# Gate and up stage of a gated feed-forward block: casts and first sums taken from GpSimd, one product copied by ScalarE, one weight load later

## The chip, the cores and the metric

The kernel runs on one core of a Trainium2 chip as one launch. The metric is the device time of one execution in microseconds (us). The times of the kernel before are the median of three runs. One further execution was taken by the hardware profiler, and all durations and start times below come from that one, counted from the start of its span.

TensorE does the matrix products and writes into PSUM banks. VectorE (DVE in the trace), ScalarE (ACT) and GpSimd (POOL) work on SBUF tiles, and DVE and ACT also read PSUM. SyncE (SP) issues the DMAs. Each engine takes its instructions in program order, and an instruction whose inputs aren't there holds up what stands behind it on that engine.

## The reference, cut to what matters

Two encoder layers over 1024 tokens of width 1024. Each has a mixer (attention), a layer norm, the feed-forward block below, a second layer norm and a gated embedding. The change lies in the first half of the feed-forward block, in both layers:

```python
def conv_ffn(x, w_gate, w_up, conv_w, conv_b, w_down):
    a = x @ w_gate                    # 1024 x 2816
    u = x @ w_up                      # 1024 x 2816
    c = conv_b                        # plus a convolution of width 3 over tokens
    for j in range(3):
        c = c + conv_w[j] * ap[:, j:j + S]    # ap: a, padded by one token
    return (gelu(c) * u) @ w_down
```

## The kernel before, in words

**Products.** Each matrix product is done in three matmuls (lines 159 to 161), since every operand is split into a rounded high part and the low rest: high by high, high by low, low by high. The high part is a cast (`CAST` on ACT, `TENSOR_SCALAR` on POOL), the low part is a subtraction on DVE (line 142).

**Seven products.** Gate and up are done as 2 x 2 blocks with seven block products in place of eight (the Strassen-Winograd scheme). A weight set, `Weights`, holds two 128-column strips of one matrix; the sets alternate, gate (even m) and up (odd m), and there are 22 in a layer (m = 0 to 21). From its quarters a00, a01, a10, a11 come four sums: the first sums s1 = a10 + a11 and s3 = a00 - a10, and, on DVE, s2 = s1 - a00 and s4 = a01 - s2. Each of a00, s2, s3, s1, a01, a11, s4 is split (14 instructions of 128x512 a set, seven casts and seven subtractions). Here `split` sends the casts of s3, a01 and a11 to POOL and the other four to ACT, and `steps` puts the two first sums on POOL for all sets from the third on (m >= 2).

**Products on TensorE.** `Products.product` issues 12 matmuls of 128x512 for one block. a00 and s2 go into the two halves of one PSUM tile `pa` (two banks, of which there are two such tiles), the others each into one of four banks `pb`. `read` sums finished blocks: m is a copy of a00's product (ACT, line 1342), u2 = m + s2's, u3 = u2 + s3's, then c11 and so on, on DVE (line 1332). A bank comes free for a later product when the last sum that reads it is done.

**The first pair.** Sets 0 and 1 are ready before the inputs are all there, and run `ahead`: their products come in the order a00, a01, then s1, s4, s2, s3, a11 for both sets by turns. So u2 of these two sets, which reads s2's half of `pa`, is due late, beside the last splits of the inputs (`xt.finish`, 128x1024 instructions on DVE and ACT). c11's second half of the work (line 1353) is one addition a set on POOL.

**Order.** `ffn` issues everything by a counter n of products; in the dictionary of line 1503 stand the steps at which a piece of `todo` (sums, then seven splits) is taken for set 2. A scheduler then fixes each engine's order from the program. Weights come by DMA on SP's queue (`load`, two of 512 KB), into a ring of 36 units that the sums and u tiles share.

Of the kernel before, what the change touches and what calls it, by code (L numbers as in the profile page):

```python
# [12 lines left out]
ALU = mybir.AluOpType  # L13
# [19 lines left out]
def tile_hybrid_encoder(  # L33
# [32 lines left out]
    nc = tc.nc  # L66
# [12 lines left out]
    def unit(s, shape, dt=F32):  # L79
        return up.tile(shape, dt, tag="u", name=nm(s))  # L80
# [26 lines left out]
    def rtile(s, shape, dt=F32R):  # L107
        return region[0].tile(s, shape, dt)
# [7 lines left out]
    def mid2(s, shape, dt=F32):  # L116
        return sm.tile(shape, dt, tag="mid2", name=nm(s), bufs=4)
# [10 lines left out]
    def f32(ap):  # L128
        return ap.bitcast(F32)
# [8 lines left out]
    def pool_copy(o, i):  # L138
        nc.gpsimd.tensor_scalar(o, i, 1.0, 1.0, op0=ALU.mult, op1=ALU.mult)  # L139

    def lo_part(lo, src, hi):
        nc.vector.tensor_tensor(lo, src, f32(hi), op=ALU.subtract)  # L142

    def split(raw, h, l, hi=None, lo=None):
        if hi is nc.scalar:
            nc.scalar.copy(h, raw)  # L146
        else:
            pool_copy(h, raw)
        (lo or nc.vector).tensor_tensor(l, raw, f32(h), op=ALU.subtract)  # L149

    def load_split(dram, shape, s, make=runit, hi=None, lo=None):
        r = region[0].raw(s + "r", shape)
        nc.sync.dma_start(out=r, in_=dram)
        h, l = make(s + "h", shape), make(s + "l", shape)
        split(r, h, l, hi, lo)
        return h, l
# [161 lines left out]
    def add(o, a, b, op=ALU.add, eng=None):  # L318
        return (eng or nc.vector).tensor_tensor(f32(o), f32(a), f32(b), op=op)

    def split_value(v, h, l, hi=None):
        if hi is nc.gpsimd:
            pool_copy(h, v)
        else:
            nc.scalar.copy(h, v)  # L325
        lo_part(l, v, h)
# [316 lines left out]
    class BlockB:  # L643
# [7 lines left out]
        def steps(self):  # L651
            out = []
            if self.pr % 2 == 0:
                out += [self.g.load] + [lambda t=t: self.g.project(t) for t in range(NT)]
            out.append(self.load)
            out += [lambda t=t: self.project(t) for t in range(NT)]
            return out
# [249 lines left out]
    class MixTiles:  # L907
# [4 lines left out]
        def seven(self, t):  # L912

            mr = region[0].raw("mr", [P, NK, P])
            nc.sync.dma_start(out=mr[:, 0:7, :], in_=mix[self.i].rearrange("k p q -> p k q")[:, 0:7, t * P:(t + 1) * P])
            two = [runit("mhl", [P, 2, 4, P]) for _ in range(2)]
            for j, m in enumerate(two):
                n = 4 - j
                split(mr[:, 4 * j:4 * j + n], m[:, 0, 0:n], m[:, 1, 0:n])
            self.m[t] = mr, two  # L920
# [342 lines left out]
    class Weights:  # L1263
# [22 lines left out]
            for step in steps:  # L1286
                step()

        HI = {"s3", "a01", "a11"}

        def split(self, name, raw=None):
            raw = name in ("a00", "a01") if raw is None else raw
            hl = region[0].raw("w", [P, 2, 4, P], F32R) if raw else rtile("w", [P, 2, 4, P])
            self.h[name], self.l[name] = hl[:, 0], hl[:, 1]
            split_value(self.v[name], hl[:, 0], hl[:, 1], nc.gpsimd if name in self.HI else None)

        def steps(self):

            return [lambda: self.sums(nc.gpsimd)] + [lambda n=n: self.split(n) for n in Products.ORDER]

    class Products:

# [26 lines left out]
        def read(self):  # L1329

            def plus(o, a, name):
                nc.vector.tensor_tensor(o, a, self.o[name], op=ALU.add)  # L1332
            out = []
            had = set(x for x, _ in self.sums)
            for name, need in list(self.sums):
                before = {"m": (), "u2": ("m",), "u3": ("u2",), "c11": ("u3",), "c00": ("m",) if self.ahead else ("u2",), "c10": ("u3", "c11"), "k5": (),
                          "c01": ("c11",)}[name]
                if any(x not in self.o for x in need) or any(x in had for x in before):
                    continue
                if name == "m":  # L1340
                    self.m = mid2("m", [P, 512])
                    nc.scalar.copy(self.m, self.o["a00"])
                elif name == "u2":
                    u = unit("u", [P, 2, 512])
                    self.u2, self.u3 = u[:, 0, :], u[:, 1, :]
                    plus(self.u2, self.m, "s2")
                elif name == "u3":
                    plus(self.u3, self.u2, "s3")
                elif name == "k5":
                    self.c11 = mid2("c11", [P, 512])  # L1350
                    nc.scalar.copy(self.c11, self.o["s1"])
                elif name == "c11" and self.ahead:
                    nc.gpsimd.tensor_tensor(self.u2, self.u2, self.c11, op=ALU.add)
                    nc.vector.tensor_tensor(self.c11, self.u3, self.c11, op=ALU.add)
                elif name == "c11":
                    self.c11 = mid2("c11", [P, 512])
                    plus(self.c11, self.u3, "s1")
                    plus(self.u2, self.u2, "s1")
                elif name == "c00":
                    if self.c00 is None:  # L1360
                        self.c00 = self.m
                    plus(self.c00, self.m, "a01")
                elif name == "c10":
                    plus(self.u3, self.u3, "a11")
                    self.c10 = self.u3
                elif name == "c01":
                    plus(self.u2, self.u2, "s4")
                    self.c01 = self.u2
                had.discard(name)
                out.append(name)  # L1370
            self.sums = [x for x in self.sums if x[0] in had]
            return out
# [14 lines left out]
    def ffn(i, w, xt, late, prefetch):  # L1387
# [3 lines left out]
        def new_c():  # L1391
            late_c.append(big("c", [P, 2, 1024]))
# [51 lines left out]
        def finished(n):  # L1444
            if n >= 0:
                m = order[n][0]
                for name in pr[m].read():
                    use(pr[m], m, name)
# [12 lines left out]
        todo = []  # L1461
        for n, (m, name) in enumerate(order):
            finished(n - 1)
            pr[m].product(name)
            if n == 0:
                c00 = unit("c00", [P, 2, 512])
                for a in range(2):
                    pr[a].go_ahead(c00[:, a])
                for a in range(2):
                    sums[a] = w[a].sums()  # L1470
                    sums[a][0]()
                    w[a].split("s1")
            if n == 1:
                late()
                new_c()
                temps = [late_c[0][:, a, :].rearrange("p (k q) -> p k q", k=2) for a in range(2)]
            if n == 2:
                for a in range(2):
                    sums[a][1]()
                    sums[a][2]()  # L1480
                    w[a].split("s4")
            if n == 3:
                for a in range(2):
                    xt.finish("t2", a)
                for a in range(2):
                    w[a].split("s2", True)
            if n == 4:
                for a in range(2):
                    xt.finish("t3", a)
                for a in range(2):  # L1490
                    sums[a][3]()
                    w[a].split("s3")
            if n == 5:
                for a in range(2):
                    xt.finish("t4", a, temps[a])
            if n == 6:
                w[0].split("a11")
                w[1].split("a11")
                w[2].load()
            if n == 7:  # L1500
                w[3].load()
                todo = w[2].steps()
            for _ in range({8: 1, 10: 2, 11: 1, 12: 1, 13: 3}.get(n, 0)):
                todo.pop(0)()
            if m >= 2 and m + 1 < NF:
                j = Products.ORDER.index(name)
                if j == 0:
                    todo = w[m + 1].steps()
                    todo[0]()
                    if m + 2 < NF:  # L1510
                        w[m + 2].load()
                todo[j + 1]()
            if m == NF - 1:
                down.ahead(Products.ORDER.index(name))
# [98 lines left out]
    for i in range(2):  # L1613
        if i == 0:
            w, mt, oT = mixer_ab(xt)
        else:
            tc.keep_in_program_order(nc.scalar.preload_act_table_set("natural_log_exp_and_others"))
            w, mt, oT = mixer_c(xt, late)
# [107 lines left out]
```

## Time and profile before

| | us |
|---|---|
| median of three runs (lowest, highest) | 3049.84 (3045.6, 3051.87) |
| the profiled execution, its own time | 3047.42 |
| its span, first to last instruction | 3045.1 |
| mean granted TensorE clock | 0.993 of full speed |
| gate and up stage, both layers together (815 to 1232 and 2300 to 2718) | 835.0, of it TensorE busy 808.9 |

The time of an execution is its span and some 2.3 us around it. In a row of a timeline the first number is the start, the second the duration; consecutive instructions of one engine overlap a little, so that the distance from start to start is shorter than the duration. "[9.24 <-DVE u L1332]" means that the engine sat idle for 9.24 us before, and that an instruction of DVE at line 1332, which writes a tile u, ended that. Tiles in the trace carry no numbers: `pa<-xb,w` is a matmul into a tile pa from an input tile and a weight tile.

### The profile page before, as it was taken

To read this page: it belongs to the slowest core of one execution; us is meant where nothing else is said; L and a number is where in the kernel's file an instruction comes from. 1 tells how busy PE (TensorE), PEld (TensorE's weight loads), DVE (VectorE), ACT (ScalarE), POOL (GpSimd) and SP (SyncE) were. 2 spreads that over 40 slices of the span, in tenths; PEclk is the share of its full clock that TensorE was granted. 3 is DMA by queue.
4 is the path that set the end of the run, shared out by engine and by line. 5 is a ranking of instruction groups with operands and counts; after the bars stand their busy time and mean duration, and the time that the engine had idled before them with its cause. 6 is when DMAs were issued, how large, how long until landed. Compare 5 with 4: busy or idle time off the path is not lost.

```text
span 3045.1 us, 42940 instructions
## 1 busy us (share of the span) xinstructions
PE 2949.2 (97%) x15456; PEld 2533.8 (83%) x15456; DVE 2308.2 (76%) x4022; ACT 1318.1 (43%) x2806; POOL 963.6 (32%) x1484
## 2 busy tenths in 40 slices
PE   8999999999989999999999999999998999999999
PEld 7888989887768888888888999998776788888887
DVE  6666477876898888688648777777769888877874
ACT  4555477761222222345225555555413222234431
POOL 4444544243232222000225555554332222210012
PEclk9999999999999999999999999999999999999999
DMA  3000100034223332734111100001431333346331
GB/s 123 29 28 19 38 29 8 8 130 134 90 98 104 104 104 100 276 133 169 63 59 34 34 32 29 28 18 56 155 129 69 115 104 104 104 163 244 115 127 66
DMA packets 119715, 272.10 MB, mean 89 GB/s; under 512 B 11344, under 2 KB 35024, under 8 KB 119504
## 3 DMA queue, kind: packets, MB, share of 16 engines
q1 hardware_dynamic: 119504, 269.37, 26.0%
q8 instruction: 122, 2.00, 0.3%
q14 instruction: 89, 0.73, 0.1%
HBM read 196.46 MB, written 72.88 MB: 88 GB/s over the span
## 4 chain that ended last, share of the span: by engine, by line
PE 74%; DVE 15%; ACT 3%; issue 3%; POOL 3%; DMA 2%; SPq 0%; DVEq 0%; ACTq 0%; POOLq 0%
PE pb L159 5%; PE pb L161 5%; PE pb L160 5%; PE xt L164 5%; PE pp L159 4%; PE s L588 4%; PE pp L161 4%; PE pp L160 4%; PE pd L159 4%; PE pd L161 4%; PE pd L160 4%; PE pa L159 2%; PE pg L159 2%; PE pg L161 2%; PE pg L160 2%
## 5 line engine op out<-in xcount | busy, mean ns | idle before, releaser
L142 DVE TENSOR_TENSOR ptl<-xt,pth 128x512 fp32r<-128x512 f32 (+2 forms) x384 | 239.7, 652 | 60.2 <-ACT pth L399 43.6
L159 PE MATMUL pp<-wh,xth 128*128 128x384 f32 x768 | 266.1, 347 | 8.0 <-ACT wh L146 7.6
L160 PE MATMUL pp<-wl,xth 128*128 128x384 f32 x768 | 258.8, 337 | 2.0 <-DVE wl L149 1.8
L161 PE MATMUL pp<-wh,xtl 128*128 128x384 f32 x768 | 257.9, 336 | 0.0
L440 ACT ACTIVATE e<-s,nmx 128x1024 f32<-128x1024 f32 x192 | 214.7, 1120 | 81.7 <-DVE nmx L838 59.0
L160 PE MATMUL pd<-wd,gd 128*128 128x512 f32 x616 | 239.9, 389 | 0.2 <-DVE wd L142 0.2
L159 PE MATMUL pd<-wd,gd 128*128 128x512 f32 x616 | 239.8, 389 | 0.0
L161 PE MATMUL pd<-wd,gd 128*128 128x512 f32 x616 | 239.7, 389 | 0.0
L325 ACT CAST w<-ws 128x512 fp32r<-128x512 f32 x132 | 81.1, 621 | 336.6 <-PE pb L161 281.0
L164 PE MATMUL xt<-ident,e 128*128 128x128 f32 x1440 | 198.1, 274 | 9.6 <-POOL e L740 3.0
L159 PE MATMUL pb<-xt,w 128*128 128x512 f32 x528 | 207.1, 392 | 0.0
L160 PE MATMUL pb<-xt,w 128*128 128x512 f32 x528 | 206.9, 392 | 0.0
L161 PE MATMUL pb<-xt,w 128*128 128x512 f32 x528 | 206.6, 391 | 0.0
L1149 ACT CAST gd<-gr 128x512 fp32r<-128x512 f32 x154 | 96.0, 623 | 214.9 <-PE pd L161 176.1
L164 PEld LDWEIGHTS xt<-ident,e 128*128 128x128 f32 x1440 | 163.5, 141 | 30.4 <-ACT sq L870 5.9
L896 POOL TENSOR_SCALAR rs<-mv 128x1 f32<-128x1 f32 x32 | 9.3, 291 | 547.7 <-DVE mv L895 547.1
L139 POOL TENSOR_SCALAR w<-ws 128x512 fp32r<-128x512 f32 x44 | 33.4, 760 | 467.0 <-PE pa L161 416.8
L142 DVE TENSOR_TENSOR gd<-gr,gd 128x512 fp32r<-128x512 f32 x154 | 106.1, 689 | 77.1 <-ACT gd L1149 77.1
L142 DVE TENSOR_TENSOR w<-ws,w 128x512 fp32r<-128x512 f32 x176 | 152.4, 870 | 5.2 <-ACT w L325 3.1
L159 PEld LDWEIGHTS pp<-wh,xth 128*128 128x128 f32 x768 | 144.6, 188 | 13.3 <-ACT wh L146 8.2
L838 DVE TENSOR_REDUCE nmx<-s 128x1 f32<-128x1024 f32 x128 | 150.4, 1214 | 2.6 <-PE s L588 2.6
L159 PE MATMUL pb<-xb,w 128*128 128x512 f32 x352 | 139.9, 397 | 9.8 <-DVE u L1332 5.7
(292 smaller groups left out, 8905.2 us busy)
## 6 DMA issues: line engine op xcount, KB each, us to landing
gr<-gated SPq DMA_DIRECT2D x76, 512.0 KB, 3.7
gated<-c SPq DMA_DIRECT2D x90, 256.0 KB, 3.5
wf<-in_w_gate_dram SPq DMA_DIRECT2D x44, 512.0 KB, 4.1
wf<-in_w_up_dram SPq DMA_DIRECT2D x44, 512.0 KB, 4.2
wd<-in_w_down_dram SPq DMA_DIRECT2D x44, 512.0 KB, 5.5
wr<-in_w_c_dram SPq DMA_DIRECT2D x32, 384.0 KB, 3.3
gated<-u SPq DMA_DIRECT2D x44, 256.0 KB, 2.2
pes<-peo SPq DMA_DIRECT2D x64, 128.0 KB, 1.9
```

The lines of the kernel that those rows point to most:

```text
L139: nc.gpsimd.tensor_scalar(o, i, 1.0, 1.0, op0=ALU.mult, op1=ALU.mult)
L142: nc.vector.tensor_tensor(lo, src, f32(hi), op=ALU.subtract)
L159: nc.tensor.matmul(o, lhsT=lh, rhs=rh, start=start, stop=False)
L160: nc.tensor.matmul(o, lhsT=lh, rhs=rl, start=False, stop=False)
L161: nc.tensor.matmul(o, lhsT=ll, rhs=rh, start=False, stop=stop)
L164: nc.tensor.transpose(o, in_=i, identity=ident)
L325: nc.scalar.copy(h, v)
L440: nc.scalar.activation(dst, s, AF.Exp, bias=negmax, scale=1.0, accum_out=l)
L588: nc.tensor.matmul(s[:, kh * 512:kh * 512 + 512], lhsT=qt[:, hl, i, :], rhs=self.ks[kh][:, j, :], start=hl == 0, stop=hl == 1)
L838: nc.vector.tensor_reduce(out=nmx, in_=s, axis=AX.X, op=ALU.max, negate=True)
L896: nc.gpsimd.tensor_scalar(rs, mv[:, 1:2], 1.0, LN_EPS, op0=ALU.mult, op1=ALU.add)
L1149: nc.scalar.copy(g[:, 0], rg)
```

## The change

Five edits, all in the gate and up stage. (1) `split` casts on ACT in all cases. (2) `steps` takes an engine: the first sums of sets 2 and 3 are done by DVE, those of later sets by POOL as before. (3) In the first pair, u2 is first a copy by ACT of s2's product, to which DVE adds m. (4) The addition of the first pair at line 1353 goes from POOL to DVE. (5) Set 3 is loaded at n = 10 in place of 7, behind the first steps of set 2.

```diff
--- before.py
+++ after.py
@@ -1286,17 +1286,15 @@
             for step in steps:
                 step()
 
-        HI = {"s3", "a01", "a11"}
-
         def split(self, name, raw=None):
             raw = name in ("a00", "a01") if raw is None else raw
             hl = region[0].raw("w", [P, 2, 4, P], F32R) if raw else rtile("w", [P, 2, 4, P])
             self.h[name], self.l[name] = hl[:, 0], hl[:, 1]
-            split_value(self.v[name], hl[:, 0], hl[:, 1], nc.gpsimd if name in self.HI else None)
-
-        def steps(self):
-
-            return [lambda: self.sums(nc.gpsimd)] + [lambda n=n: self.split(n) for n in Products.ORDER]
+            split_value(self.v[name], hl[:, 0], hl[:, 1])
+
+        def steps(self, eng):
+
+            return [lambda: self.sums(eng)] + [lambda n=n: self.split(n) for n in Products.ORDER]
 
     class Products:
 
@@ -1343,14 +1341,18 @@
                 elif name == "u2":
                     u = unit("u", [P, 2, 512])
                     self.u2, self.u3 = u[:, 0, :], u[:, 1, :]
-                    plus(self.u2, self.m, "s2")
+                    if self.ahead:
+                        nc.scalar.copy(self.u2, self.o["s2"])
+                        add(self.u2, self.u2, self.m)
+                    else:
+                        plus(self.u2, self.m, "s2")
                 elif name == "u3":
                     plus(self.u3, self.u2, "s3")
                 elif name == "k5":
                     self.c11 = mid2("c11", [P, 512])
                     nc.scalar.copy(self.c11, self.o["s1"])
                 elif name == "c11" and self.ahead:
-                    nc.gpsimd.tensor_tensor(self.u2, self.u2, self.c11, op=ALU.add)
+                    nc.vector.tensor_tensor(self.u2, self.u2, self.c11, op=ALU.add)
                     nc.vector.tensor_tensor(self.c11, self.u3, self.c11, op=ALU.add)
                 elif name == "c11":
                     self.c11 = mid2("c11", [P, 512])
@@ -1498,14 +1500,15 @@
                 w[1].split("a11")
                 w[2].load()
             if n == 7:
+                todo = w[2].steps(nc.vector)
+            if n == 10:
                 w[3].load()
-                todo = w[2].steps()
             for _ in range({8: 1, 10: 2, 11: 1, 12: 1, 13: 3}.get(n, 0)):
                 todo.pop(0)()
             if m >= 2 and m + 1 < NF:
                 j = Products.ORDER.index(name)
                 if j == 0:
-                    todo = w[m + 1].steps()
+                    todo = w[m + 1].steps(nc.vector if m == 2 else nc.gpsimd)
                     todo[0]()
                     if m + 2 < NF:
                         w[m + 2].load()
```

ScalarE in layer one, from the last casts of the inputs on. In the program order before (xt are inputs, w weights of set 2 and ws their sums, c_10441 a scratch tile that then holds gate values):

```order
L325 CAST xt_2492_10513<-t_2426_10113 128x1024
L325 CAST xt_2498_10540<-c_10441 128x1024
L1399 ACTIVATE c_10441<-c_2464_10384,convt 128x512
L325 CAST xt_2500_10546<-c_10441 128x1024
L325 CAST w_10641<-wf_10573 128x512
L325 CAST w_10644<-ws_10606 128x512
L325 CAST w_10694<-ws_10606 128x512
```

and after, where w_10518 to w_10570 belong to sets 0 and 1, and pa_10371 and pa_10443 hold s2's products of these:

```order
L325 CAST w_10518<-ws_10386 128x512
L325 CAST w_10522<-ws_10392 128x512
L325 CAST w_10567<-wf_10261 128x512
L325 CAST w_10570<-wf_10296 128x512
L325 CAST xt_2498_10540<-c_10441 128x1024
L1401 ACTIVATE c_10441<-c_2464_10384,convt 128x512
L325 CAST xt_2500_10546<-c_10441 128x1024
L325 CAST w_10643<-wf_10573 128x512
L325 CAST w_10720<-wf_10573 128x512
L325 CAST w_10646<-ws_10602 128x512
L1345 COPY u_10608<-pa_10371 128x512
L1345 COPY u_10623<-pa_10443 128x512
```

Five of these casts came from POOL (w_10518, w_10522, w_10567, w_10570 and w_10720). All stand ahead of the cast of set 2's s2 (w_10646), and behind that stand the two copies out of PSUM.

VectorE at the same place, from the low parts of set 2's first weights on. Before (u is u2 of sets 0 and 1, pb_10628 s3's product):

```order
L142 TENSOR_TENSOR w_10718<-wf_10573,w_10718 128x512
L142 TENSOR_TENSOR w_10641<-wf_10573,w_10641 128x512
L319 TENSOR_TENSOR ws_10606<-ws_10606,wf_10573 128x512
L319 TENSOR_TENSOR ws_10607<-wf_10573,ws_10606 128x512
L1332 TENSOR_TENSOR u_10612<-m_10397,pa_10371 128x512
L1332 TENSOR_TENSOR u_10626<-m_10466,pa_10443 128x512
L142 TENSOR_TENSOR w_10644<-ws_10606,w_10644 128x512
L1332 TENSOR_TENSOR u_10612<-u_10612,pb_10628 128x512
```

and after:

```order
L142 TENSOR_TENSOR w_10643<-wf_10573,w_10643 128x512
L142 TENSOR_TENSOR w_10720<-wf_10573,w_10720 128x512
L319 TENSOR_TENSOR ws_10602<-wf_10574 128x512
L319 TENSOR_TENSOR ws_10603<-wf_10573,wf_10574 128x512
L319 TENSOR_TENSOR ws_10602<-ws_10602,wf_10573 128x512
L319 TENSOR_TENSOR ws_10603<-wf_10573,ws_10602 128x512
L142 TENSOR_TENSOR w_10646<-ws_10602,w_10646 128x512
L319 TENSOR_TENSOR u_10608<-u_10608,m_10397 128x512
L319 TENSOR_TENSOR u_10623<-u_10623,m_10466 128x512
L1330 TENSOR_TENSOR u_10608<-u_10608,pb_10626 128x512
```

The two first sums are new here, and the additions into u read no PSUM.

VectorE some 30 instructions on, where set 3 is made. Before (pb_10785 is s3's product of set 2):

```order
L319 TENSOR_TENSOR ws_10753<-ws_10753,wf_10590 128x512
L319 TENSOR_TENSOR u_10626<-c_10441,u_10626 128x512
L319 TENSOR_TENSOR ws_10754<-wf_10590,ws_10753 128x512
L142 TENSOR_TENSOR w_10763<-wf_10590,w_10763 128x512
L142 TENSOR_TENSOR w_10780<-ws_10753,w_10780 128x512
L142 TENSOR_TENSOR w_10798<-ws_10754,w_10798 128x512
L142 TENSOR_TENSOR w_10815<-ws_10753,w_10815 128x512
L1332 TENSOR_TENSOR u_10783<-m_10766,pa_10740 128x512
L142 TENSOR_TENSOR w_10834<-wf_10590,w_10834 128x512
L1332 TENSOR_TENSOR u_10783<-u_10783,pb_10785 128x512
```

and after (pb_10787 is that product):

```order
L319 TENSOR_TENSOR ws_10755<-wf_10640 128x512
L319 TENSOR_TENSOR u_10623<-c_10441,u_10623 128x512
L319 TENSOR_TENSOR ws_10755<-ws_10755,wf_10639 128x512
L319 TENSOR_TENSOR ws_10756<-wf_10639,wf_10640 128x512
L319 TENSOR_TENSOR ws_10756<-wf_10639,ws_10755 128x512
L142 TENSOR_TENSOR w_10765<-wf_10639,w_10765 128x512
L142 TENSOR_TENSOR w_10782<-ws_10755,w_10782 128x512
L1330 TENSOR_TENSOR u_10785<-m_10768,pa_10742 128x512
L142 TENSOR_TENSOR w_10800<-ws_10756,w_10800 128x512
L1330 TENSOR_TENSOR u_10785<-u_10785,pb_10787 128x512
```

Two first sums came in, two low parts went behind, and the read of s3's product still ends the piece. On TensorE the product behind it, set 2's s4, is issued after ten matmuls of set 3's a00 in place of four.

## Rows read from the trace of the kernel before

**Rows 1.** The page: busy time by engine (1), the chain by engine (4).
```profile
PE 2949.2 (97%) x15456; PEld 2533.8 (83%) x15456; DVE 2308.2 (76%) x4022; ACT 1318.1 (43%) x2806; POOL 963.6 (32%) x1484
...
PE 74%; DVE 15%; ACT 3%; issue 3%; POOL 3%; DMA 2%; SPq 0%; DVEq 0%; ACTq 0%; POOLq 0%
```

**Rows 2.** TensorE's waits, whole program: line, releaser, us in total, times, longest.
```profile
PE pa L159 <- DVE u L1332: 18.5, 2, 9.2
...
PE pb L159 <- DVE u L1332: 5.7, 2, 2.9
...
PE pa L159 <- ACT m L1342: 1.7, 4, 0.5
```

**Rows 3.** Windows, layer one: engines' busy us (instructions), granted clock, DMA share, GB/s.
```profile
839.00:848.20 9.20, 0.05 (x1) 0.00 (x0) 9.07 (x10) 3.52 (x5) 4.85 (x4) 0.77 0.01 3
848.20:854.10 5.90, 5.81 (x14) 4.34 (x15) 5.33 (x8) 0.54 (x1) 2.90 (x2) 0.50 0.01 3
854.10:873.90 19.80, 19.80 (x88) 16.12 (x86) 19.80 (x28) 8.53 (x12) 5.86 (x5) 1.00 0.26 96
873.90:881.30 7.40, 4.54 (x14) 3.42 (x14) 7.40 (x12) 2.33 (x3) 3.09 (x2) 0.78 0.69 251
...
882.00:1218.00 336.00, 334.80 (x1462) 272.81 (x1462) 291.47 (x423) 95.97 (x140) 88.79 (x86) 1.00 0.30 102
```

**Rows 4.** Timeline of TensorE around both gaps: start us, duration us, line, form, [idle before].
```profile
838.66 0.39 PE L161 MATMUL pb<-xt,w 128*128 128x512 f32 x1
848.29 0.77 PE L159 MATMUL pa<-xb,w 128*128 128x512 f32 x1 [9.24 <-DVE u L1332]
...
873.67 0.39 PE L159 MATMUL pa<-xb,w 128*128 128x512 f32 x1
876.91 0.50 PE L159 MATMUL pb<-xb,w 128*128 128x512 f32 x1 [2.86 <-DVE u L1332]
```

**Rows 5.** Timeline of VectorE over the same stretch, layer one.
```profile
829.25 1.29 DVE L319 TENSOR_TENSOR ws<-wf,wf 128x512 f32<-128x512 f32 x2
830.45 1.22 DVE L319 TENSOR_TENSOR c<-xb,t 128x1024 f32<-128x1024 f32 x1
832.18 2.12 DVE L142 TENSOR_TENSOR w<-ws,w 128x512 fp32r<-128x512 f32 x2 [0.51 <-POOL w L139]
...
837.93 2.31 DVE L142 TENSOR_TENSOR xt<-c,xt 128x1024 fp32r<-128x1024 f32 x1
...
843.56 1.46 DVE L142 TENSOR_TENSOR xt<-c,xt 128x1024 fp32r<-128x1024 f32 x1
...
846.14 0.68 DVE L319 TENSOR_TENSOR ws<-ws,wf 128x512 f32<-128x512 f32 x1
...
847.46 1.28 DVE L1332 TENSOR_TENSOR u<-m,pa 128x512 f32<-128x512 f32 x2
...
851.71 1.75 DVE L1354 TENSOR_TENSOR c<-u,c 128x512 f32<-128x512 f32 x1 [0.57 <-POOL u L1353]
...
870.96 1.09 DVE L319 TENSOR_TENSOR u<-c,u 128x512 f32<-128x512 f32 x1
...
876.19 0.67 DVE L1332 TENSOR_TENSOR u<-u,pb 128x512 f32<-128x512 f32 x1
```

**Rows 6.** The tile ws, GpSimd's groups: duration ns min/median/max, first and last.
```profile
L139 POOL TENSOR_SCALAR w<-ws x22: 620/620/2030, 830.1 to 1216.1; 128x512 fp32r<-128x512 f32 x22
L319 POOL TENSOR_TENSOR ws<-wf x20: 1287/1292/1724, 837.5 to 1197.7; 128x512 f32<-128x512 f32 x20
```

**Rows 7.** Timeline of ScalarE: casts, then the copy of m in the steady part.
```profile
822.16 1.14 ACT L325 CAST w<-ws 128x512 fp32r<-128x512 f32 x2
...
842.48 1.04 ACT L325 CAST xt<-c 128x1024 fp32r<-128x1024 f32 x1 [1.39 <-DVE c L319]
...
1038.50 0.58 ACT L1342 COPY m<-pa 128x512 f32<-128x512 f32 x1
```

**Rows 8.** Timeline of TensorE: the product behind that copy.
```profile
1039.13 0.50 PE L159 MATMUL pa<-xt,w 128*128 128x512 f32 x1
```

## The prediction

> **What bounds the kernel now.** I read the page first. TensorE is busy 97% of the span and carries 74% of the chain that ended last, VectorE (DVE) 15% [rows 1]. So time is won only where TensorE stands still. Its waits come next: over the whole program the largest is a matmul into pa behind a DVE addition into u, 9.2 us twice, and in the same form on pb 2.9 us twice, once in each layer [rows 2]. In the steady part of the stage TensorE hardly waits: for ScalarE's (ACT's) copy m of a00's product it lost 1.7 us in four waits in the whole program [rows 2].
>
> The timeline puts the two waits where set 2 starts. TensorE issues the last product of the first pair's s3 at 838.66 and stands until 848.29; it stands again from 873.9 until 876.91 [rows 4]. Behind both gaps the granted clock is 0.50 of full speed for a while (1.2 in place of 2.4 GHz): 14 matmuls took 5.9 us, where 88 at full clock took 19.8, 0.225 us each [rows 3]. So the first gap costs 9.24 us and 5.90 - 14 x 0.225 = 2.75 us of slow matmuls, the second 2.86 and (7.40 - 2.86) - 14 x 0.225 = 1.39 us.
>
> DVE has no hole in the first gap: busy 9.07 of 9.20 us [rows 3]. The matmul waits for the additions u = m + s2's product at 847.46, the last readers of pa [rows 5], and these stand at the end of a queue. That queue is slow beside GpSimd (POOL): a 128x1024 subtraction takes 1.22 us at 830.45 and 2.31 at 837.93, two of 128x512 take 1.29 at 829.25 and 2.12 at 832.18 [rows 5].
>
> **The change part by part.** Casts to ACT and no POOL work in the start-up. From 832.18 to 843.56 eight DVE instructions in seven rows are stretched over their lengths elsewhere (0.68 and 1.22) by 4.46 us in all, and there is 0.51 us of waiting for a POOL cast [rows 5]. Both go, since POOL then has nothing to do there. I walk DVE's new list from 829.25. Ahead of that only the casts of a01 of sets 0 and 1 move to ACT, with no reader waiting there; were one late, it would cost a cast's 0.52. Start to start it takes 0.60 us for 128x512 (829.25 to 830.45 for two) and 1.14 for 128x1024. Two sums, a 1024, two low parts, two 1024, a low part, two 1024, a low part: 6 x 0.60 + 5 x 1.14 = 9.30, so 838.55. The next waits for ACT: its cast can start when the second-last 1024 ends (838.03) and takes 1.04 [rows 7], so DVE goes on at 839.2, one 1024 (840.35), the low parts of set 2's a00 and a01 (841.55), the two first sums that came from POOL (842.75), then the s2 sum. This was at 846.14 [rows 5]; it ends at 843.45.
>
> ACT's five added casts before that cost nothing: four run at 0.52 us start to start [rows 7] from 830.0, when ACT is idle, and are done by 832.2, ahead of DVE's need at 831.6 for the first; a01's runs while DVE has a 1024. ACT then casts s2 (0.52) and copies pa (0.58, by the copy m out of the same tile [rows 7]): 844.55. From the end of DVE's read (848.14) to the matmul at 848.29 were 0.15 us [rows 4, 5]. So TensorE starts at 844.7 and not at 848.29: **3.56 us** less. The two u additions stay on DVE, now from SBUF, at the 0.68 of the s2 sum, but nothing in pa waits for them. After four matmuls TensorE wants the bank of the first s3 product, which DVE reads behind s2's low part and two u additions, done at 846.6, against 846.4: **0.33** lost with the 0.15.
>
> Here a page speaks to the size of the stretch. The rows show that DVE lost 4.46 us [rows 5] beside seven POOL casts and two first sums, which take 0.62 and 1.29 us at their shortest [rows 6], 6.9 us in all. The Trainium skill (SBUF — State Buffer, Who interferes with whom) says that a DVE instruction with two SBUF inputs and a GpSimd instruction that reads SBUF lock each other out for a whole instruction. By that DVE could have lost up to 6.9 us, and freeing it would bring the restart forward by up to 2.4 us more. The trace decides for 4.46, and the walk above needs neither.
>
> The gap is then 844.7 - 838.9 = 5.8 us. The clock fell behind gaps of 2.86 and of 9.24, so I leave the 2.75 us of slow matmuls as they are.
>
> The second gap. It ended when DVE had read set 2's s3 product at 876.19 [rows 5]. From the s2 sum (846.14) that is 30.05 us of list. Six of its rows (851.71 the first, 870.96 the last) are stretched by 4.1 us in sum, and 0.57 is a wait for POOL's u [rows 5]. The new list has two more instructions in this piece: the two u additions of line 1355 and set 3's two first sums came in, and two low parts went behind. So 30.05 - 4.7 + 1.2 + 0.2 for waits on ACT = 26.8, from 842.75: start 869.5, bank free 870.3. TensorE comes to it after the 25.6 us that it had from 848.29 to 873.9, and six more matmuls (1.36): 844.7 + 0.3 + 25.6 + 1.4 = 872.0. With 1.7 us in hand the gap goes: **2.86 and 1.39 us**.
>
> What else moves. Set 3's load goes behind two steps of set 2, but on SP's queue it is still ahead of the first spill of gated values, and its first reader on DVE (ws_10755) comes at about 864, some 20 us behind the restart; that covers it, and if it is late, set 3 is late by as much. In sets 4 to 21 three casts a set go to ACT, which is busy 96.0 of 336 us there [rows 3]; POOL keeps the first sums, so DVE gains little, and TensorE has only 1.7 us to gain. Nothing of it counts.
>
> Sum for a layer: 3.56 - 0.33 + 2.86 + 1.39 = 7.5 us; the waits are the same in the other layer [rows 2]: **15.0 us**. The profiled execution took 3047.42, so 3032.4; the median lies 2.42 above it, so **3034.8** for the median.
>
> **The rivals.** *The second wait stays.* The hand of 1.7 us rests on a walk over 43 instructions; a cast late on ACT takes it. Especially the cast of set 3's a01, which waits for set 2's a01 product, stands ahead of set 3's s2 cast, whose low part stands ahead of the bank's reader. Against it: that product ends 5 us before TensorE's need, and cast, cast and four DVE instructions take some 3.7. Then the gain is 3.23 x 2 = 6.5 and 3043.3.
>
> *The clock stays up* in the shorter first gap. Against it: it fell behind 2.86 us [rows 3]. Then 2.75 x 2 more: 3029.3.
>
> *The copies come no sooner* (the change doesn't do what it says). They are behind a cast that waits for DVE's s2 sum, so ACT can be ready long before and frees nothing; if DVE's rate doesn't recover without POOL, its two added sums take 1.2 us and the restart is at 848 or later, and only part of the second gap goes: 0 to 4 us, 3047.8 at 2.
>
> *Slower: ACT late in the steady part.* The second product of every set, s2 into pa, waits until ACT has copied m. That copy starts at 1038.50, ends at 1039.08, and the matmul starts at 1039.13 [rows 7, 8]: no time in hand. ACT is in order, and the three new casts each wait for a buffer that TensorE must have done with. If one holds up the chain to this copy by a cast's length (0.62) in each of 18 sets in two layers, 36 x 0.62 = 22.3 us go: 3034.8 + 22.3 = 3057.1. It decides from 15.0 / 36 = 0.42 us a set. For it: there is no slack. Against it: the added casts wait for products two or more ahead of the set's end, and ACT is idle over two thirds of that time [rows 3]; in the order nothing was put between the cast of the next a00 and the copy.
>
> **How the numbers follow.** Forecast 0.62; second wait stays 0.15; clock up 0.07; no sooner 0.08; slower 0.08. The low end, 3027, takes in the clock case with one us more in each layer; the high end, 3046, takes in the second wait and the better half of the copies' case, and leaves out some 0.14. A measurement of this kernel can tell 0.2%, 6.1 us, from no change, so faster is below 3043.7: forecast, clock, and three quarters of the second wait, 0.80; same 0.12; slower 0.08.
>
> **What would show it.** Right: TensorE waits once for ACT's copy into u, for some 5.8 us, starts about 3.5 us sooner, and the wait of 2.9 is gone; DVE's 128x1024 instructions there take 1.2 us each. Wrong: a wait on pb near the start of set 3's first product, or waits for m above 0.1 us in every set, or stretched DVE rows with POOL idle.

## The result and the profile after

The changed kernel takes 3032.64 us (median of four runs, 3027.25 to 3035.44) against 3049.27 for the kernel before beside it (3045.6 to 3051.87): a ratio of 0.9942, 95% interval 0.993 to 0.9955, or 16.6 us less, where 3034.8 was predicted. A second measurement, below, gave 3033.69 against 3049.31. The profiled execution took 3031.43 with a span of 3029.7.

The busy line and the chain by engine, from the page, answer to [rows 1]. GpSimd lost 108 us of work and ScalarE took 82; VectorE, with 12 instructions more, is busy 22 us less.

```profile
PE 2948.5 (97%) x15456; PEld 2537.0 (84%) x15456; DVE 2286.5 (75%) x4034; ACT 1400.4 (46%) x2942; POOL 855.1 (28%) x1340
...
PE 78%; DVE 12%; ACT 3%; issue 2%; DMA 2%; POOL 2%; SPq 0%; DVEq 0%; ACTq 0%; POOLq 0%
```

TensorE's waits over the whole program (us in total, times, longest), against [rows 2]: the pa wait ends with ScalarE's copy and is 5.5 in place of 9.2, the pb wait of 2.9 is gone, and the copy of m holds TensorE twice for 1.7 in place of four times for 1.7 together.

```profile
PE pa L159 <- ACT u L1345: 11.0, 2, 5.5
...
PE pa L159 <- ACT m L1340: 3.2, 2, 1.7
```

The windows of layer one show the same as [rows 3]: a gap with VectorE full, 13 matmuls at the low clock, and then, where the second gap was, TensorE without a hole (31.30 of 31.30).

```profile
839.40:845.00 5.60, 0.12 (x1) 0.00 (x0) 5.37 (x8) 2.33 (x6) 0.00 (x0) 0.89 0.30 94
845.00:850.70 5.70, 5.68 (x13) 4.02 (x14) 5.70 (x11) 3.20 (x6) 0.00 (x0) 0.51 0.32 95
850.70:882.00 31.30, 31.30 (x140) 25.91 (x139) 30.93 (x49) 14.84 (x21) 3.03 (x3) 1.00 0.36 126
882.00:1218.00 336.00, 334.32 (x1463) 272.97 (x1462) 286.23 (x423) 128.96 (x193) 59.03 (x34) 1.00 0.31 106
```

TensorE's timeline, against [rows 4]: the last product ahead of the gap, the restart, the first matmul into pb, the bank that the second gap waited for (871.97, no wait), and a wait that the kernel before does not have. This one stands in set 5's second product, while the weights of set 6 are made; it is called the wait at set 6 below. It is 1.68 us here and 1.47 in layer two.

```profile
839.13 0.39 PE L161 MATMUL pb<-xt,w 128*128 128x512 f32 x1
845.02 0.79 PE L159 MATMUL pa<-xb,w 128*128 128x512 f32 x1 [5.50 <-ACT u L1345]
...
847.06 0.80 PE L159 MATMUL pb<-xt,w 128*128 128x512 f32 x1
...
871.97 0.39 PE L159 MATMUL pb<-xb,w 128*128 128x512 f32 x1
...
916.85 0.50 PE L159 MATMUL pa<-xt,w 128*128 128x512 f32 x1 [1.68 <-ACT m L1340]
```

VectorE's timeline, against [rows 5]: every 128x1024 row takes 1.21 to 1.23, GpSimd is idle beside it, and the s2 sum starts at 843.15 in place of 846.14.

```profile
836.13 1.21 DVE L142 TENSOR_TENSOR xt<-c,xt 128x1024 fp32r<-128x1024 f32 x1
...
839.60 1.23 DVE L142 TENSOR_TENSOR xt<-c,xt 128x1024 fp32r<-128x1024 f32 x1 [0.52 <-ACT xt L325]
...
843.15 0.68 DVE L319 TENSOR_TENSOR ws<-ws,wf 128x512 f32<-128x512 f32 x1
...
870.23 0.68 DVE L1330 TENSOR_TENSOR u<-u,pb 128x512 f32<-128x512 f32 x1
```

### The profile page after: what moved, and what is told of

The parts are those of the page before. It is cut to its first block, busy times and chain, and to the rows that moved or that the text cites. A ratio compares the mean times of both kernels' runs of the same rounds, so it can differ in the third digit from the quotient of the medians.

```text
span 3029.7 us, 42896 instructions
## 1 busy us (share of the span) xinstructions
PE 2948.5 (97%) x15456; PEld 2537.0 (84%) x15456; DVE 2286.5 (75%) x4034; ACT 1400.4 (46%) x2942; POOL 855.1 (28%) x1340
## 4 chain that ended last, share of the span: by engine, by line
PE 78%; DVE 12%; ACT 3%; issue 2%; DMA 2%; POOL 2%; SPq 0%; DVEq 0%; ACTq 0%; POOLq 0%
PE pb L159 6%; PE pb L160 6%; PE pb L161 6%; PE xt L164 5%; PE pp L159 4%; PE pp L160 4%; PE pp L161 4%; PE pd L161 4%; PE pd L160 4%; PE pd L159 4%; PE s L588 4%; PE pa L159 2%; PE pa L161 2%; PE pa L160 2%; PE pg L159 2%
## 5 line engine op out<-in xcount | busy, mean ns | idle before, releaser
L319 POOL TENSOR_TENSOR ws<-wf 128x512 f32<-128x512 f32 x36 | 65.3, 1815 | 564.3 <-DMA gated<-u 200.0
L325 ACT CAST w<-ws 128x512 fp32r<-128x512 f32 x176 | 107.9, 621 | 213.3 <-PE pb L161 128.1
L325 ACT CAST w<-wf 128x512 fp32r<-128x512 f32 x132 | 80.9, 619 | 183.9 <-PE pb L161 128.7
L159 PEld LDWEIGHTS pp<-wh,xth 128*128 128x128 f32 x768 | 145.3, 189 | 13.3 <-ACT wh L146 8.5
L160 PEld LDWEIGHTS pp<-wl,xth 128*128 128x128 f32 x768 | 145.5, 189 | 4.7 <-DVE wl L149 4.5
```

The lines of the kernel that those rows point to most:

```text
L159: nc.tensor.matmul(o, lhsT=lh, rhs=rh, start=start, stop=False)
L160: nc.tensor.matmul(o, lhsT=lh, rhs=rl, start=False, stop=False)
```

## The experiments

The theory that went into them: VectorE's list sets both gaps, and GpSimd's work beside it makes that list slow; the other edits are worth little by themselves. The rivals give the gain to ScalarE's copies, to the first sums, or to the later load.

**Each part by itself.** e1 lets VectorE read pa as before:

```diff
-                    if self.ahead:
-                        nc.scalar.copy(self.u2, self.o["s2"])
-                        add(self.u2, self.u2, self.m)
-                    else:
-                        plus(self.u2, self.m, "s2")
+                    plus(self.u2, self.m, "s2")
```

> The changed kernel, but VectorE reads pa itself for the second products of the first pair (u = m + product, as before) in place of ScalarE's copies. My theory (GpSimd out of the start-up is what counts): VectorE's s4 sum ends at 844.5, so its two additions end at 845.2 and 845.8 and TensorE starts again at 845.3 in place of 845.02; the reads of pb behind them stay where they are (846.3) and there is no second gap. Total 0.6 us over the changed kernel's, so within 2 us of it. Rival (ScalarE's copies free pa, and that is the gain): the restart goes back by most of its 3.7 us in each layer, 5 to 7 us over the changed kernel.

3032.38 us, ratio 0.9943 (0.9928 to 0.9958); gap 5.77 in place of 5.50, in TensorE's timeline:

```profile
847.11 0.77 PE L159 MATMUL pa<-xb,w 128*128 128x512 f32 x1 [5.77 <-DVE u L1330]
```

ScalarE's copies are worth 0.3 us a layer. The rival falls.

e2 is the kernel before with the casts taken from GpSimd and nothing else:

```diff
-            split_value(self.v[name], hl[:, 0], hl[:, 1], nc.gpsimd if name in self.HI else None)
+            split_value(self.v[name], hl[:, 0], hl[:, 1])
```

> The kernel before, with the casts of s3, a01 and a11 on ScalarE and nothing else; the first sums of all sets and the additions of the first pair's c11 stay on GpSimd, VectorE reads pa. My theory: of GpSimd's work in the start-up, two first sums are left (2.6 us at their shortest), which stretch VectorE by some 1.7 us and take 1.2 from it: restart 0.5 to 1 us later than in the changed kernel, the second gap under 0.5: 1 to 3 us over the changed kernel, 12 to 15 under the one before. Rival (all parts are needed, above all the first sums and additions taken from GpSimd): the second gap of 2.9 us stays in each layer, and at most half of the 15 us is gained.

3032.96 us, ratio 0.9948 (0.9933 to 0.9963): one edit has the whole gain, within what can be told. Its profiled execution took 3040.2, some 7 us over the other three, so only waits and rows are read from it. TensorE's waits (us in total, times, longest) differ:

```profile
PE pa L159 <- DVE u L1332: 12.2, 2, 6.1
...
PE pb L159 <- DVE u L1332: 3.4, 2, 1.7
...
PE pa L159 <- ACT m L1342: 0.4, 2, 0.2
```

The first gap is 0.6 longer than after the full change, as expected; 1.7 us of the second gap are left, where under 0.5 was expected; and the new wait at set 6 is not there: TensorE comes to that place 73.8 us behind the restart, in place of 71.8 with the wait, and ScalarE's copy is just done. What edits 2 to 5 win at the second gap they lose at set 6. Beside the two first sums that are left on GpSimd, VectorE's rows in the timeline, 1.23 and 1.29 alone, read:

```profile
840.59 1.71 DVE L142 TENSOR_TENSOR xt<-c,xt 128x1024 fp32r<-128x1024 f32 x1 [0.52 <-ACT xt L325]
842.22 2.35 DVE L142 TENSOR_TENSOR w<-wf,w 128x512 fp32r<-128x512 f32 x2
```

and GpSimd's first sum, 1.29 us at its shortest:

```profile
837.79 3.43 POOL L319 TENSOR_TENSOR ws<-wf 128x512 f32<-128x512 f32 x1 [31.26 <-DMA wf<-in_w_gate_dram]
```

The rows of VectorE ahead of its idle 0.52 kept their lengths, and GpSimd's sum lasted until behind that hole; the rows behind it are the long ones. They lost 0.48 + 1.06 = 1.54 us for two sums that cost VectorE 1.20 if it does them itself.

e7 is the reverse, the changed kernel with the casts back on GpSimd (`split_value(..., nc.gpsimd if name in ("s3", "a01", "a11") else None)`).

> The changed kernel with the casts of s3, a01 and a11 back on GpSimd in all sets; the first sums, ScalarE's copies and the later load stay as changed. My theory: seven casts (4.3 us at their shortest) stretch VectorE by some 2.8 us, with 0.5 of waiting: restart 3 us later in each layer, second gap under 0.6: 6 to 8 us over the changed kernel. Rival (the first sums and copies carry the gain, the casts are hidden): within 2 us of the changed kernel.

3046.27 us, ratio 0.9991 (0.9981 to 1.0): without the casts' move the other four edits are worth 3 us. The gap is 7.73, 2.2 longer than after, and 2.15 of that are 1.64 of stretched rows and a wait of 0.51, all beside five casts. VectorE's timeline of e7, the last two rows with GpSimd idle again:

```profile
831.65 2.10 DVE L142 TENSOR_TENSOR w<-ws,w 128x512 fp32r<-128x512 f32 x2 [0.51 <-POOL w L139]
833.67 1.62 DVE L319 TENSOR_TENSOR c<-c,xb 128x1024 f32<-128x1024 f32 x1
835.22 1.63 DVE L319 TENSOR_TENSOR c<-xb,t 128x1024 f32<-128x1024 f32 x1
...
836.77 0.68 DVE L142 TENSOR_TENSOR w<-wf,w 128x512 fp32r<-128x512 f32 x1
837.37 1.21 DVE L142 TENSOR_TENSOR xt<-c,xt 128x1024 fp32r<-128x1024 f32 x1
```

I had 3 us from VectorE's loss over GpSimd's shortest times, all kinds in one ratio; the two sums of e2 cost VectorE 0.77 each, these casts 0.33. The total, 13.6 over the changed kernel, is more than the 6 to 8 expected: TensorE's waits for m come to 7.2 us in seven places, where the changed kernel has 3.2 in two. That is read from the fastest of ten executions (3041.32); what the others lost beyond it isn't shown.

e4 puts set 3's load back to `n == 7`.

> The changed kernel with the load of set 3 issued ahead of set 2's steps again, as before the change. On every engine and queue the instructions stand in the same order as in the changed kernel, so theory: nothing changes, within 1 us. Rival (the later load takes other buffers, and that is what frees set 3's first sums): a wait before 876 that the changed kernel does not have.

3029.87 us (two runs, 3025.49 and 3034.25, too far apart to tell 2 us), gap 5.49, wait at set 6 1.56: in the waits the later load changes nothing.

**GpSimd busy, nobody reading its results.** e3 lets GpSimd read the values that it used to cast (without the a01 of sets 0 and 1; those of these two sets twice) in pieces of 128x128, and write a constant:

```diff
+            if self.spare and name in ("s3", "a11", "a01"):
+                for j in (0, 1, 2, 3) * self.spare:
+                    nc.gpsimd.tensor_scalar(ones, self.v[name][:, j], 0.0, 1.0, op0=ALU.mult, op1=ALU.add)
```

> The changed kernel, and in the start-up GpSimd reads the values s3 and a11 of sets 0 and 1 (twice) and s3, a11, a01 of set 2 (once) in pieces of 128x128 and writes a constant over a constant; no instruction of another engine waits for it, and the other engines' instructions stand in the same order. My theory (GpSimd's work slows VectorE's instructions beside it, some 0.65 us for each us of it): VectorE's 128x1024 rows of the start-up take up to 2.3 us again, the restart comes 3 to 5 us later in each layer, and the second gap may come back: 6 to 11 us over the changed kernel. Rival (VectorE's queue lost time to waits for GpSimd's results and to its place in the order, not to GpSimd's work beside it): the rows stay at 1.21, and the time within 1 us of the changed kernel's.

3046.47 us, ratio 0.999 (0.998 to 0.9999), a time over the one expected and for another reason. VectorE's long rows stayed at 1.22 to 1.23; VectorE then stood still, in its timeline:

```profile
841.16 1.22 DVE L142 TENSOR_TENSOR xt<-c,xt 128x1024 fp32r<-128x1024 f32 x1 [0.51 <-ACT xt L325]
...
845.10 0.69 DVE L319 TENSOR_TENSOR ws<-wf 128x512 f32<-128x512 f32 x1 [1.33 <-POOL ones L1296]
848.65 0.69 DVE L319 TENSOR_TENSOR ws<-wf,wf 128x512 f32<-128x512 f32 x1 [2.85 <-POOL ones L1296]
```

for this row of GpSimd:

```profile
832.04 16.57 POOL L1296 TENSOR_SCALAR ones<-ws 128x128 f32<-128x128 f32 x16 [24.94 <-DVE ws L319]
```

The new ws tiles take the buffers that GpSimd was still reading: 4.2 us of waiting, which I had ruled out. So the time proves nothing about slower rows, though by itself it would have passed for a proof. The sixteen pieces are not alike either. In the view of the tile the first alone (ns: shortest, median, longest) took 8.76 us of the 16.57:

```profile
L1296 POOL TENSOR_SCALAR ones<-ws x1: 8759/8759/8759, 832.0 to 832.0; 128x128 f32<-128x128 f32 x1
```

It ended at 840.80, in VectorE's idle 0.51 ahead of 841.16. Until then VectorE's rows kept their lengths with GpSimd held up; behind that, one more long row kept 1.22, and two of 128x512 at 842.30 took 1.47 for 1.29.

e9 repeats it with less: each value once, in two pieces of 128x256, into an unused tile.

```diff
+            if self.spare is not None and name in ("s3", "a11", "a01"):
+                for j in (0, 2):
+                    pool_copy(self.spare, self.v[name][:, j:j + 2])
```

> The changed kernel, and in the start-up GpSimd casts the seven values that it cast before (s3 and a11 of sets 0 and 1, s3, a11 and a01 of set 2; of sets 0 and 1 the a01s are left out), each in two pieces of 128x256, into a tile that nobody reads; the other engines' instructions stand in the same order. In e7_pool_casts the same seven casts took 2.1 to 2.8 us from VectorE and moved the restart by 2.2. Theory (casts beside VectorE stretch its instructions): rows of 128x1024 over 1.5 us again beside them, restart 1.5 to 2.5 us later than in the changed kernel, 3 to 7 us in all. Rival (a GpSimd instruction with one input slows VectorE only where VectorE waits for its result or its buffer, as the 128x128 pieces of e3_idle_pool left the rows at 1.22): rows of 1.21, time within 1.5 us of the changed kernel's.

3037.63 us, ratio 0.996 (0.9944 to 0.9975): 5.0 over the changed kernel, 3.9 over its second measurement. The gap is 6.54, and a wait of 0.59 at pb follows, 1.46 more in each layer than after the full change. The timeline of VectorE:

```profile
834.99 1.22 DVE L319 TENSOR_TENSOR c<-xb,t 128x1024 f32<-128x1024 f32 x1
...
840.20 1.31 DVE L142 TENSOR_TENSOR xt<-c,xt 128x1024 fp32r<-128x1024 f32 x1 [0.51 <-ACT xt L325]
841.43 1.68 DVE L142 TENSOR_TENSOR w<-wf,w 128x512 fp32r<-128x512 f32 x2
843.03 0.88 DVE L319 TENSOR_TENSOR ws<-wf 128x512 f32<-128x512 f32 x1
```

and that of GpSimd beside it, with its first piece alone, in the view of the tile:

```profile
831.09 11.48 POOL L139 TENSOR_SCALAR nat<-ws 128x256 fp32r<-128x256 f32 x4 [24.92 <-DVE ws L319]
842.65 3.12 POOL L139 TENSOR_SCALAR nat<-wf 128x256 fp32r<-128x256 f32 x4
...
L139 POOL TENSOR_SCALAR nat<-ws x1: 8864/8864/8864, 831.1 to 831.1; 128x256 fp32r<-128x256 f32 x1
```

No row waits for GpSimd, and yet nine 128x512 additions and subtractions take up to 0.88 in place of 0.68: so its work beside them costs time by itself. Half of the expectation failed: the 128x1024 rows kept 1.22, but for the last, with 1.31. Beside them GpSimd's first piece took 8.86 us, to 839.95, and so ended in VectorE's idle 0.51 ahead of 840.20, as in e3; all the longer rows stand behind that hole.

**The copies' place.** e8 has ScalarE's two copies ahead of the cast of set 2's s2, for which they waited 3 us (shown without the line that notes the second copy):

```diff
+            if n == 10:
+                todo.pop(0)()
+                with tc.issue_after(pr[1].freed.ins):
+                    todo.pop(0)()
```

> The changed kernel with ScalarE's two copies out of pa ahead of the cast of set 2's s2, for which they waited some 3 us (that cast waits for VectorE's sum). Theory: TensorE is then held by the low part of set 2's a00 alone: restart 2.5 to 3.1 us sooner, gap 2.4 to 3 in place of 5.5; VectorE's list is not shortened, so the bank of the first s3 product of set 2 is free where it was, TensorE comes to it 3 us sooner and waits 1.3 to 1.7 there: 1.4 us gained in each layer, 3 in all (0 if the clock falls again behind the second gap, 8 if it no longer falls behind the first). Rival (the copies were not what held the restart): gap 5.5 as before, no change.

3029.99 us, ratio 0.9933 (0.9921 to 0.9945). The gap moved, as TensorE's timeline shows:

```profile
840.71 0.50 PE L159 MATMUL pa<-xb,w 128*128 128x512 f32 x1 [1.58 <-ACT u L1345]
846.59 0.80 PE L159 MATMUL pb<-xt,w 128*128 128x512 f32 x1 [4.23 <-DVE u L1330]
```

1.58 + 4.23 = 5.81 against 5.50 + 0.17. Six matmuls later TensorE wants the bank of the first pair's s3 product, which VectorE reads where it always did. The copies held the restart and nothing else; I had forgotten that bank, which the prediction named. Whatever opens pa, VectorE's list closes the stretch.

**The wait at set 6.** Half of that set's load is issued behind four spills, at 900.41. I took this for the cause; e6 issues each load ahead of the first sums (`w[m + 2].load()` above `todo = ...`).

> The changed kernel with each load of weights of the steady part issued ahead of that set's first sums in the program, so that both halves of set 6's load stand ahead of the spills of gated values on SyncE's queue. Theory (half of that load sits behind the spills, and GpSimd's first sum, the low parts, the gelu and the copy of m follow late): the wait of 1.7 us in each layer for m at set 6 goes, and no other comes: 3.4 us under the changed kernel. Rival (the chain to m is late for another reason, as GpSimd's slower first sums or VectorE's order): the wait stays, time within 1 us; or the loads wait for free buffers and hold up the spills: slower.

3045.42 us, ratio 0.9979 (0.9971 to 0.9988), and my reading falls: both halves are issued from 881.65 on, GpSimd's sum starts at 904.69 (904.42 after the full change) because it waits for VectorE's low part, and the wait stays at 1.54. What the sum brings with it shows after the full change, in a row of VectorE and one of ScalarE:

```profile
906.18 1.77 DVE L319 TENSOR_TENSOR ws<-ws,wf 128x512 f32<-128x512 f32 x1 [1.19 <-POOL ws L319]
...
916.22 0.57 ACT L1340 COPY m<-pa 128x512 f32<-128x512 f32 x1
```

VectorE waits 1.19 for GpSimd's sum and then loses 1.09 beside the next one, 2.28 in all; its work for the gelu ends late, the gelu too, and the copy of m stands behind it. GpSimd's timeline in e6:

```profile
904.69 1.30 POOL L319 TENSOR_TENSOR ws<-wf 128x512 f32<-128x512 f32 x1 [12.10 <-DVE w L142]
```

and TensorE's:

```profile
915.83 0.50 PE L159 MATMUL pa<-xt,w 128*128 128x512 f32 x1 [1.54 <-ACT m L1340]
```

The loss of 12.8 us is mostly waits for m, 13.3 us in 16 places in place of 3.2 in two: with the load, other instructions of VectorE changed places. Which of them matters I did not settle.

e10 takes GpSimd out altogether (`todo = w[m + 1].steps(nc.vector)` for every m); the changed kernel ran once more beside it, and e13 joins e8 and e10.

> The changed kernel once more, beside the next two on the same chip. Expected of any theory: 3030 to 3035, with the wait of 5.5 us for ScalarE's copy and that of 1.7 for m at set 6 in each layer. The difference between this and the first measurement is what a comparison across calls is worth.

> The changed kernel with the first sums of all sets on VectorE, so that GpSimd does nothing in the gate and up stage. In e2_casts_only two first sums on GpSimd took 1.55 us from VectorE; the two cost it 1.2 when it does them itself. Theory (GpSimd's sums cost VectorE more than they spare it): VectorE's busy time from set 3 to the stage's end falls a little or stays, its waits for GpSimd of 1.2 to 1.5 us go, and with them TensorE's wait of 1.7 us at set 6: 2 to 4 us under e0_after_again. Rival (GpSimd's first sums spare VectorE work in the steady part): VectorE's list gets longer, the copies of m come late in more sets, slower than e0_after_again by over 2 us.

> e8_copy_first and e10_sums_dve together: ScalarE's copies out of pa ahead of set 2's cast, and no work on GpSimd in the gate and up stage. In e8 the gap only moved (1.6 us at pa and 4.2 at pb, 5.8 in all, in place of 5.5 and 0.2), but 7 matmuls ran slow behind it in place of 13, about 1.2 us a layer. Theory: the two gains add, 4 to 6 us under e0_after_again. Rival (the copies' place is worth nothing, as its timing of 3030.0 could also be the changed kernel's): no more than e10_sums_dve.

e0: 3033.69 us, ratio 0.9948 (0.9935 to 0.996), 1.05 above its first median, so a difference below that between two measurements says nothing. e10: 3027.3, ratio 0.9924 (0.9912 to 0.9937), 6.4 under e0. e13: 3028.74, ratio 0.9933 (0.9919 to 0.9946): e8's place for the copies adds nothing, and its rival is right. In a window of 336 us with nearly the same work TensorE has no hole left in e10. The changed kernel again (engines' busy us and instructions, clock, DMA share, GB/s):

```profile
882.00:1218.00 336.00, 334.36 (x1464) 273.04 (x1463) 285.64 (x424) 128.33 (x192) 59.40 (x34) 1.00 0.32 106
```

and in e10, with GpSimd at nothing:

```profile
879.00:1215.00 336.00, 336.00 (x1472) 274.51 (x1471) 288.76 (x461) 130.07 (x194) 0.00 (x0) 1.00 0.31 106
```

VectorE does 37 instructions more there, 22 us at 0.60, and is busy only 3.1 longer: 34 sums on GpSimd had stretched it by some 19 us, 0.56 each, and its waits for them are gone too. TensorE's waits explain 3.2 of the 6.4 us. From the restart to the first matmul of the down stage e10 takes 842.19 to 1234.29, 392.10, and e0 846.29 to 1240.23, 393.94: 1.84 less. In layer two it is 391.37 against 394.42, 3.05 less, of which 1.4 are a shorter slow stretch behind the first gap (6 matmuls against 13). That makes 4.9; where the other 1.5 us come from isn't shown.

e14 is the kernel before with two edits alone, the casts as in e2 and `self.sums(nc.vector)` in `steps`.

> The kernel before with two edits alone: the casts of s3, a01 and a11 on ScalarE, and the first sums of all sets on VectorE. The first pair's additions of c11 stay on GpSimd, VectorE reads pa itself, the load of set 3 stays early. Theory (what costs is GpSimd's work beside VectorE; ScalarE's copies and the later load are worth nothing by themselves): gap of 5.8 us as in e1_u2_by_dve, no wait of 1.7 at set 6; in e2_casts_only the additions of c11 took 1.65 us from VectorE where the two would cost it 1.2, so the bank that the second gap waits for is free 0.4 later, with some 1.4 in hand: no second gap. 3027 to 3030, as e10_sums_dve within 2 us. Rival (the additions of c11 on GpSimd are what left e2_casts_only its second gap of 1.7 us): the gap stays, 3 to 6 us over e10_sums_dve.

3027.99 us, ratio 0.9922 (0.9909 to 0.9936), gap 5.75, no second gap, no wait at set 6; TensorE's waits in the stage are these:

```profile
PE pa L159 <- DVE u L1332: 11.5, 2, 5.7
...
PE pa L159 <- ACT m L1342: 1.1, 1, 1.1
```

The 1.1 us come once, in layer two, for m of set 2, some 9 us after VectorE has waited 0.59 for GpSimd's addition of c11 and lost 1.09 in a row beside the next; whether that is the cause isn't shown. Two of the five edits, the second carried to all sets, reach the time of the best version, without the copies, the move of c11's additions or the load's new place.

## Why the prediction was right, step by step

- *Restart.* 844.7 was predicted, 845.02 came, with the stretch starting 0.47 later (839.13 for 838.66). Gap against gap it is 9.24 - 5.50 = 3.74 us for 3.56. The walk over VectorE's list held row by row (s2 sum to end at 843.45; it ended at 843.83). Its cause is shown: the casts alone take the gap from 9.24 to 6.10 in e2 and from 5.50 to 7.73 in e7, and e9 moves it by 1.04 without any wait for GpSimd.
- *The copies.* "ACT then casts s2 and copies pa" was so; that they matter was not claimed, and e1 puts them at 0.3.
- *New wait for the pb bank.* 0.33 predicted, 847.06 - 846.46 - 0.43 = 0.17 measured; e8 shows that this bank is the real end of the gap.
- *Slow clock.* 13 matmuls in 5.70 us at granted 0.51: 5.70 - 13 x 0.225 = 2.78, for 2.75 left unchanged. The rival with the clock up falls.
- *Second gap.* Gone. The bank's reader started at 870.23 (869.5 predicted), 0.4 of that from the later s2 sum, so that TensorE could go on at 871.06 (870.3); it came at 871.97 (872.0). 0.9 us were in hand for 1.7. In e2 the gap came back with 1.74. In the kernel before, the clock fell only some five matmuls behind this gap (near 877.95), and not right behind it, as the prediction reads; its 1.39 us hold.
- *The steady part.* "Nothing of it counts" was wrong, though it came out near nothing: a wait came at set 6 in each layer (1.68 and 1.47), and four of 0.30 to 0.54 went. The slower rival named this very wait, ScalarE's copy of m; it came in one set of a layer, not in eighteen, and behind GpSimd's sums, not behind added casts: e10 and e14, without these sums, don't have it. That the loss stayed at 0.7 us a layer is luck: the prediction has no row on GpSimd's sums there.
- *The sum.* Waits that went: (18.5 + 5.7 + 1.7) - (11.0 + 3.2 + 0.35) = 11.35; the second slow stretch 2 x 1.39 = 2.8; 14.1 of the 15.4 us by which the spans differ, for 15.0 predicted.

On the lock of the Trainium skill (SBUF — State Buffer, Who interferes with whom): the up to 2.4 us more that it left open did not come. By it either engine blocks for the other's whole instruction. The rows show both sides held up, but not by that length: VectorE lost 0.41 a row beside casts of 0.62 and 0.20 a row in e9 beside pieces of 0.72, and GpSimd's first piece in e9 took 8.86, longer than several rows of VectorE.

## What to carry to other kernels

Where VectorE's queue ends a wait of TensorE, look first at what GpSimd does beside it: an operation moved there can cost VectorE as much as doing it, or more (1.54 for 1.20 in the start-up, 0.56 for 0.60 a sum behind it). Ask of a chain of edits which one carries the gain; here two do, and one of them had been stopped short. And where a wait is taken away, name the next reader on the same list: e8 opened one bank and stood at the next.

## What the runs showed of the hardware

- What VectorE pays beside GpSimd is not set by the form of their instructions alone. While VectorE went from row to row without a hole, GpSimd's first instruction beside it was held up: 8.86 us for a cast of 128x256 in e9, 8.76 for a read of 128x128 in e3, 3.43 for a 128x512 sum in e2. Each ended in or just behind VectorE's next idle 0.51 or 0.52. Behind that hole VectorE lost time: 0.41 in each 128x1024 addition beside casts of 128x512 (e7, where the hole was its own wait for such a cast), 0.20 in a 128x512 row beside casts of 128x256 (e9). That the hole lets GpSimd in is a reading of these rows; no run moved it. It isn't needed everywhere: in the kernel before a first sum that came at 837.54 took 1.61, and VectorE's row at 837.93 lost 1.09 at once. What decides stays open.
- Not every gap of TensorE brings the low clock (granted 0.5, 1.2 GHz). Behind 1.74 us in e2 the first matmuls ran at 1.00 and those from 875.20 to 878.40 at 0.52; behind 1.68 after the full change it stayed at 1.00 (916.85 to 922.00). Behind 4.23 it was 0.52 for eight (e8), behind 9.24 in the kernel before 0.50. The six matmuls at 1.00 behind e8's 1.58 decide nothing, as the next gap follows them.
